# The chunk loop of an RWKV-7 recurrence, issued as eight pairs or as two groups of four

## The chip, the cores and the metric

The kernel runs on one NeuronCore of a Trainium2 chip. The metric is the device time of one execution in microseconds (us); lower is better. The engines that matter here are TensorE (PE, with its weight loads as PEld), VectorE (DVE), ScalarE (ACT), GpSimd (POOL) and the SyncE queue (SP), which issues the DMA transfers.

## The reference, cut to what matters

The model is a trunk of two layers on a sequence of 1024 positions with 1024 channels. Layer 0 mixes tokens with a chunked gMLP, layer 1 with RWKV-7 time mixing; each is followed by cross-attention into a memory and by a SwiGLU feed-forward block. The change touches only the recurrence of layer 1, for 16 heads of width 64:

```
def step(S, inp):                       # S: one 64 x 64 state for each head
    r_t, w_t, k_t, v_t, a_t, b_t = inp
    sa = einsum('bhij,bhj->bhi', S, a_t)
    S = S * w_t + sa (x) b_t + v_t (x) k_t
    return S, einsum('bhij,bhj->bhi', S, r_t)
...
y = rwkv7_recurrence(r, decay, k, v, -kk, kk * a)
y = group_norm(y) * ln_g + ln_b + sum(r * k * r_k) * v
out = (y * g) @ w_o
```

All inputs and outputs are 32-bit floats.

## The kernel before

The recurrence is computed in chunks of 64 positions. The 1024 positions are four *batches* of 256, so a batch has four chunks. Two heads share the 128 partitions and are called a *pair*, written `p`; there are eight pairs. Two pairs share their tiles and are called a *double*, written `pi`; there are four doubles. For each batch `b` there are five pieces of work, each written as a Python generator that yields between steps:

- **Preparation** (`rwkv_prep`, one call for each double): five loads from a scratch in DRAM, a scan of the decay (L1265), two exponentials (L1268, L1269), scaled operands `AR` and `BK` (L1277 to L1281, the last on POOL), a column of sums (L1288), 16 matmuls of the two operands (L1300) whose results are masked by DVE (L1303), eight transposes (L1307), the diagonal blocks stored to DRAM for the solve (L1313, L1314), a load of `v` (L1318) and 32 matmuls (L1324). Its products are four tiles `AR`, `GR`, `BT`, `UV` of the pool `A`.
- **Substitution** (`rwkv_solve`, one call for all eight pairs): a triangular inverse by forward substitution, 31 steps. Each step has one or two DVE operations (L1348), one DVE addition (L1345) and one POOL product (L1352) that need each other in turn. It begins with a load of the blocks that the preparation of all four doubles stored (L1336) and ends with stores to DRAM (L1357, L1360). Its tiles `invA` and `invZ` have one buffer each and are shared with the merge.
- **Merge** (`rwkv_merge`): loads the inverse back and joins its blocks by 32x32 matmuls (L1386, L1395) into the two tiles `Z`.
- **Chunk loop** (`rwkv_chunks`): 32 *units*, four chunks for each of eight pairs. A unit is: matmul of the state (L1422), DVE addition (L1423), matmul with `Z`, ACT copy (L1429), matmuls for the output and the new state (all recorded at L1409), ACT copy of the output (L1438) and ACT scaling of the state (L1441). The next chunk of the same pair needs the scaled state. Each unit holds one of the four PSUM banks of the pool `ck`, from its first matmul to its last copy.
- **Norm** (`rwkv_post`, one call for each double): mean, variance, scaling, transposes (L1496, L1503), gate, and a store of `z`.

The order in which the pieces are emitted is, for b = 1, 2: chunk loop of batch b-1; substitution of batch b; preparation of batch b+1 with the norm of batch b-1 ticking beside it; merge of batch b. For b = 3: chunk loop of batch 2, substitution of batch 3, then the output projection `W_o` begins; between its two column passes for the first half of the sequence come the merge of batch 3 and the chunk loop of batch 3.

The emitted order is not the order on the engines. The program is built with a planner (`schedule_with_timeline_sim=True`) that places every instruction into its engine's stream; an instruction emitted earlier has the higher priority, but one that the planner takes to be ready may be placed ahead of it. What stands in an engine's stream then runs in that order.

`stagger(gens, lag)` advances several generators in turn, the i-th from step `i * lag` on. `run` advances generators one after another and ticks the queued tasks (`later`) between steps; `drain` finishes the queued tasks.

Of the kernel before, what the change touches and what calls it, by code (L numbers as in the profile page):

```python
# [15 lines left out]
KD = D // P  # L16
# [5 lines left out]
class Trunk:  # L22
# [1375 lines left out]
            nc.scalar.copy(R['Z'][pi // 2][lo[pi], :, :, 32:64], pb[pi][lo[pi], :].rearrange('p (h c t) -> p h c t', h=2, c=8))  # L1398
            yield

    def rwkv_chunks(self, R, B, b, states):

        nc = self.nc
        heads = [slice(h * 64, h * 64 + 64) for h in range(2)]
        if b == 0:
            for p in range(KD):
                states[p] = R['st'].tile([P, P], F32, name='s', tag=f's{p}')
                nc.gpsimd.memset(states[p], 0.0)
        mm = lambda o, l, r: nc.tensor.matmul(o, lhsT=l, rhs=r, start=False, stop=True, skip_group_check=True)  # L1409

        def one(c4, p):
            pi, c = (p // 2, p % 2 * 4 + c4)
            T = B['T'][pi]
            AR, UV, BT, GR = (T['AR'], T['UV'], T['BT'], T['GR'])
            zr, to = (heads[pi % 2], heads[c % 2])
            bk = self.bank_ck()
            ar, u, sp = (bk[:, 0:128], bk[0:64, 128:256], bk[:, 256:384])
            s0 = states[p]
            last = b == 3 and c4 == 3
            rs = R['rs'][pi % 2][(p // 4 * 2 + p % 2) % 4]  # L1420
            uvc = UV[0:64, c].rearrange('i h v -> i (h v)')
            nc.tensor.matmul(ar, lhsT=AR[:, c, :, :], rhs=s0, start=True, stop=True)  # L1422
            nc.vector.tensor_add(rs[zr, :], ar[0:64, :], uvc)  # L1423
            if not last and False:
                nc.scalar.activation(s0, s0, AF.Copy, scale=T['D'][:, c:c + 1])
            yield
            for h, hs in enumerate(heads):
                mm(u[:, hs], R['Z'][pi // 2][:, h, c, :], rs[:, hs])
            nc.scalar.copy(uvc, u)  # L1429
            yield  # L1430
            if not last:
                mm(sp, self.ident, s0)
            for h, hs in enumerate(heads):
                mm(ar[64:128, hs], GR[:, h, c, :], UV[:, c, h, :])
            if not last:
                for h, hs in enumerate(heads[::-1]):
                    mm(sp[hs, hs], BT[:, c, hs], UV[:, c, hs.start // 64, :])
            e = lambda: nc.scalar.copy(AR[to, c - c % 2].rearrange('i a v -> i (a v)'), ar[64:128, :])  # L1438
            e()
            if not last:  # L1440
                nc.scalar.activation(s0, sp, AF.Copy, scale=T['D'][:, c:c + 1])  # L1441
            if not 1:
                e()
        order = sorted(((c4, p) for c4 in range(4) for p in range(KD)), key=lambda x: x[0] * 8 + x[1] + 1 * (x[1] // 2))
        if not 1:
            for c4, p in order:
                for _ in one(c4, p):
                    pass
                yield
            return  # L1450
        live = []
        for c4, p in order:
            live.insert(0, one(c4, p))
            live = [g for g in live if next(g, True) is None]
            yield
        while live:
            live = [g for g in live if next(g, True) is None]
            yield
# [50 lines left out]
    def rwkv(self, W, C, filler, mk_close):  # L1509
        nc = self.nc  # L1510
        B = [self.rwkv_batch() for _ in range(4)]
        R, states = ({}, {})
# [6 lines left out]
        def stagger(gens, lag):  # L1519

            gens = list(gens)
            done = [False] * len(gens)
            n = 0
            while not all(done):
                for i, g in enumerate(gens):
                    if n >= i * lag and (not done[i]):
                        try:
                            next(g)
                        except StopIteration:
                            done[i] = True  # L1530
                n += 1
                yield

        def prep(b):
            return stagger([self.rwkv_prep(R, B[b], pi, b, D_[0], C) for pi in range(4)], 7 if b else 6)

        def chunks(b):
            yield from self.rwkv_chunks(R, B[b], b, states)

        def post(b):  # L1540
            return stagger([self.rwkv_post(R, B[b], pi, b, D_[0], C) for pi in range(4)], 2 if b == 3 else 1)

        def run(*gens, rate=1):
            for g in gens:
                for _ in g:
                    self.tick(rate)

        def gated(half):

            xh, xl = self.chunks()  # L1550
            for k in range(KD):
                t = R['ld'].tile([P, 512], F32, name='zt', tag='ld')
                nc.sync.dma_start(t, D_[0]['z'][k, :, half * 512:half * 512 + 512])
                self.split(xh[k], xl[k], t)
            return (xh, xl)
        D_ = []

        def before_last():
            self.close_main()
            pools(left, 'left', ('inv', 1), ('D', 8))  # L1560
            self.rwkv_consts(left.enter_context(self.tc.tile_pool(name='rconst', bufs=1, reuse_waits='tile', side='left')), C)
            pools(left, 'left', ('ld', 7))
            pools(top, 'left', ('tt', 4))
            self.open_main(2, 3, 2)
            self.open_psum(4, 4)
            self.later(prep(0))
        d, gate_out = self.rwkv_project(W, C, filler, before_last, D_)
        self.drain()
        run(self.rwkv_solve(R, B[0]))
        p1 = prep(1)  # L1570
        self.later(p1)
        gate_out()
# [9 lines left out]
            nc.gpsimd.memset(z[96:128, :, :, 0:32], 0.0)  # L1582
        run(self.rwkv_merge(R, B[0]), p1)
        for b in range(1, 4):
            o = 3
            sv = self.rwkv_solve(R, B[b])
            if o in (0, 1):
                run(sv, chunks(b - 1))
            elif o in (2, 3):
                run(chunks(b - 1), sv)  # L1590
            else:
                self.later(sv)
                run(chunks(b - 1), rate=1)
                self.drain(0)
            self.later(post(b - 1), 1)
            if b == 3:
                break
            if o in (0, 2, 4):
                run(self.rwkv_merge(R, B[b]))
            run(prep(b + 1), rate=1)  # L1600
            if o in (1, 3, 5):
                run(self.rwkv_merge(R, B[b]))
            self.drain()
        top.close()
        self.open_main(2, 2, 1, 'left')
# [6 lines left out]
        x = gated(0)  # L1612

        def between():
            run(self.rwkv_merge(R, B[3]))
            self.drain()
            run(chunks(3))
            self.later(post(3), 1)
        first = self.out_half(x, 0, W['o'], close, 4, between)
        self.drain()  # L1620
        self.open_psum(8)
        x = gated(1)
# [82 lines left out]
```

## Time and profile before

| | us |
|---|---|
| median of three runs | 3295.14 (3293.02 to 3295.40) |
| the profiled execution, its own time | 3312.53 |
| span in its trace | 3310.8 |
| TensorE busy in the span | 3135.4 (95%) |
| VectorE busy | 2025.2 (61%) |
| ScalarE busy | 1490.8 (45%) |
| GpSimd busy | 1058.4 (32%) |

Mean granted TensorE clock over the span: 0.956 of full speed. The span runs from the first instruction to the last; the remaining 1.7 us of the execution's own time lie around it. Times inside the trace are counted from the span's start. The four chunk loops lie between 1884 and 2264 us. A busy TensorE is not a fast one: the column `PEclk` of the views tells which share of its full clock was granted, 1.00 for 2.4 GHz and 0.50 for 1.2 GHz.

### The profile page before, as it was taken

Reading aid. Unit: us, or ns where it says so; the run is one execution under the profiler, and the core shown is the slowest. Engines: PE = TensorE matmul, PEld = TensorE weight load, DVE = VectorE, ACT = ScalarE, POOL = GpSimd, SP = SyncE. Lnnn points to the kernel's source line nnn. Section 1 sums busy time; section 2 is a strip of 40 time slices with the busy share of each in tenths; the row PEclk is TensorE's granted clock in tenths of the full one; section 3 lists DMA queues with packets and bytes.
Section 4 is the critical chain, followed back from the end, with each engine's and each line's share of the span. In section 5 each row is a group of like instructions: output and inputs, shape, how many; then the busy total and the mean of one; then the engine's idle time right before and its main releaser. Section 6 shows DMA issues by size and latency. Waiting matters only on the chain. (4 is left out here: it accounts for less than half of the span.)

```text
span 3310.8 us, 44442 instructions
## 1 busy us (share of the span) xinstructions
PE 3135.4 (95%) x16570; PEld 2545.7 (77%) x16570; DVE 2025.2 (61%) x2876; ACT 1490.8 (45%) x2759; POOL 1058.4 (32%) x800
## 2 busy tenths in 40 slices
PE   8999999899999888999889899999999899999897
PEld 6888888778888666888667787887788688887676
DVE  5463545655444998755766567545545744445998
ACT  5443544533333433766743454445545533334332
POOL 0000011443334654311512244223011533334664
PEclk9999999999999999999999888779999999999998
DMA  5622544332222432744956644335554233323322
GB/s 186 204 77 70 197 147 141 114 96 83 77 77 85 144 102 77 238 136 131 301 173 169 169 121 100 105 92 176 178 163 150 65 96 86 86 77 120 103 96 96
DMA packets 448407, 421.97 MB, mean 127 GB/s; under 512 B 76672, under 2 KB 351264, under 8 KB 448192
## 3 DMA queue, kind: packets, MB, share of 16 engines
q1 hardware_dynamic: 441280, 393.96, 38.8%
q0 software_dynamic: 6912, 25.17, 2.4%
q8 instruction: 131, 2.15, 0.3%
q14 instruction: 84, 0.69, 0.1%
HBM read 314.13 MB, written 104.92 MB: 127 GB/s over the span
## 5 line engine op out<-in xcount | busy, mean ns | idle before, releaser
L438 PE MATMUL ps<-a,wh 128*128 128x512 f32 x2464 | 772.6, 399 | 6.1 <-DVE a L119 4.6
L119 DVE TENSOR_TENSOR wl<-wr,wh 128x1024 fp32r<-128x1024 f32 (+1 forms) x369 | 447.6, 1223 | 349.8 <-ACT wh L118 349.2
L438 PEld LDWEIGHTS ps<-a,wh 128*128 128x128 f32 x2464 | 465.6, 189 | 123.2 <-DVE a L119 7.0
L118 ACT CAST wh<-wr 128x1024 fp32r<-128x1024 f32 (+1 forms) x369 | 323.5, 889 | 522.4 <-PE ps L438 180.1
L438 PE MATMUL ps<-a,wl 128*128 128x512 f32 x1232 | 479.6, 397 | 0.0
L606 PE MATMUL ps<-wh,a 128*128 128x512 f32 x1136 | 380.3, 408 | 48.6 <-DVE a L615 32.6
L148 PE MATMUL ps<-a,wh 128*128 128x512 f32 (+1 forms) x848 | 330.3, 395 | 10.9 <-ACT a L118 5.9
L149 PE MATMUL ps<-a,wh 128*128 128x512 f32 (+1 forms) x848 | 325.7, 386 | 2.2 <-DVE a L119 2.2
L150 PE MATMUL ps<-a,wl 128*128 128x512 f32 (+1 forms) x848 | 325.4, 386 | 1.6 <-DVE wl L119 1.5
L148 PE MATMUL ps<-wh,a 128*128 128x512 f32 x800 | 313.9, 402 | 13.7 <-DVE a L1504 4.8
L149 PE MATMUL ps<-wl,a 128*128 128x512 f32 x800 | 318.5, 398 | 0.6 <-DVE wl L119 0.6
L150 PE MATMUL ps<-wh,a 128*128 128x512 f32 x800 | 316.7, 400 | 0.0
L606 PEld LDWEIGHTS ps<-wh,a 128*128 128x128 f32 x1136 | 218.9, 193 | 120.7 <-DVE a L615 32.5
L438 PEld LDWEIGHTS ps<-a,wl 128*128 128x128 f32 x1232 | 233.2, 189 | 57.6 <-DVE wl L119 0.8
L119 DVE TENSOR_TENSOR wl<-s,wh 128x512 fp32r<-128x512 f32 (+1 forms) x200 | 210.8, 1066 | 76.6 <-ACT wh L118 73.7
L118 ACT CAST wh<-s 128x512 fp32r<-128x512 f32 (+1 forms) x200 | 129.8, 662 | 251.0 <-PE ps L438 91.8
L606 PE MATMUL ps<-wl,a 128*128 128x512 f32 x568 | 228.8, 403 | 0.0
L208 POOL TENSOR_TENSOR sm<-sm,mhalf 128x4 f32<-128x4 f32 (+3 forms) x60 | 67.5, 1127 | 498.1 <-DVE sm L228 422.4
L119 DVE TENSOR_TENSOR a<-a 128x1024 fp32r<-128x1024 f32 (+1 forms) x134 | 208.1, 1567 | 24.3 <-ACT a L118 22.3
L615 DVE TENSOR_TENSOR a<-ps,a 128x512 f32<-128x512 f32 x304 | 194.8, 676 | 13.5 <-PE ps L606 13.4
L148 PEld LDWEIGHTS ps<-a,wh 128*128 128x128 f32 x848 | 163.3, 194 | 43.8 <-ACT a L118 6.8
L148 PEld LDWEIGHTS ps<-wh,a 128*128 128x128 f32 x800 | 151.9, 190 | 51.4 <-DVE a L1504 5.3
(273 smaller groups left out, 5631.7 us busy)
## 6 DMA issues: line engine op xcount, KB each, us to landing
wr<-in_ffn_w_in SPq DMA_DIRECT2D x90, 512.0 KB
scr<-t SPq DMA_DIRECT2D x136, 256.0 KB
scr<-t SPq DMA_DIRECT2D x60, 512.0 KB
a<-scr SPq DMA_DIRECT2D x108, 256.0 KB
wr<-in_rw_w_rkv SPq DMA_DIRECT2D x48, 512.0 KB
t<-scr SPq DMA_DIRECT2D x36, 512.0 KB
ld<-scr SPq DMA_DIRECT2D x72, 256.0 KB
wr<-in_xa_wkv SPq DMA_DIRECT2D x32, 512.0 KB
```

The source lines that it names most:

```text
L118: self.nc.scalar.copy(hi, src)
L119: (engine or self.nc.vector).tensor_sub(lo, src, hi)
L148: nc.tensor.matmul(out, lhsT=ah, rhs=bh, start=start, stop=False)
L149: nc.tensor.matmul(out, lhsT=ah, rhs=bl, start=False, stop=False)
L150: nc.tensor.matmul(out, lhsT=al, rhs=bh, start=False, stop=stop)
L208: self.nc.gpsimd.tensor_tensor(out=r, in0=v, in1=self.mhalf[:, 0:n], op=ALU.pow)
L438: self.nc.tensor.matmul(out, lhsT=a, rhs=b, start=start and k == 0 and (i == 0), stop=k == 3 and i == 2, skip_group_check=True)
L606: nc.tensor.matmul(ps, lhsT=a, rhs=b, start=start and k == 0 and (q == 0), stop=k == K - 1 and q == 2, skip_group_check=True)
L615: nc.vector.tensor_add(o, ps, o)
```

## The change

The chunk loop takes a group of four pairs (two doubles) and is called twice for each batch. The other work of the recurrence is emitted in turn with it, in halves of two doubles:

- With the first group of batch b-1, the preparation of doubles 2 and 3 of batch b (for b = 1 there is none, since batch 1 is already prepared).
- With the second group of batch b-1, the substitution of batch b, then side by side with it the norm of doubles 0 and 1 of batch b-1, followed by the preparation of doubles 0 and 1 of batch b+1.
- Then the norm of doubles 2 and 3 of batch b-1 is queued and the merge of batch b is emitted.
- For b = 3 whatever is left of substitution and norm when the second group ends is queued to run beside the output projection. Before the merge of batch 3 the queue is now drained first. The two groups of batch 3 are emitted in turn with each other.

No instruction's shape, engine or count changes.

```diff
+        pairs = range(4 * group, 4 * group + 4)
...
-        order = sorted(((c4, p) for c4 in range(4) for p in range(KD)), key=lambda x: x[0] * 8 + x[1] + 1 * (x[1] // 2))
+        order = [(c4, p) for c4 in range(4) for p in pairs]
...
+        def seq(*gens):
+            for g in gens:
+                yield from g
+        groups = [(0, 1), (2, 3)]
...
         for b in range(1, 4):
-            o = 3
             sv = self.rwkv_solve(R, B[b])
-                run(chunks(b - 1), sv)
-            self.later(post(b - 1), 1)
+            run(stagger([chunks(b - 1, 0), prep(b, groups[1]) if b > 1 else iter(())], 0))
+            ahead = prep(b + 1, groups[0]) if b < 3 else iter(())
+            rest = stagger([sv, seq(post(b - 1, groups[0]), ahead)], 0)
             if b == 3:
+                live = chunks(b - 1, 1)
+                for _ in live:
+                    next(rest, None)
+                self.later(rest)
+                self.later(post(b - 1, groups[1]), 1)
                 break
-            run(prep(b + 1), rate=1)
-                run(self.rwkv_merge(R, B[b]))
+            run(stagger([chunks(b - 1, 1), rest], 0))
+            self.later(post(b - 1, groups[1]), 1)
+            run(self.rwkv_merge(R, B[b]))
             self.drain()
...
         def between():
+            self.drain()
             run(self.rwkv_merge(R, B[3]))
-            self.drain()
-            run(chunks(3))
+            run(stagger([chunks(3, g) for g in range(2)], 0))
             self.later(post(3), 1)
```

## Rows read from the trace of the kernel before

**Rows 1.** Page, the span in 40 slices: TensorE busy tenths and granted clock tenths

```profile
PE   8999999899999888999889899999999899999897
...
PEclk9999999999999999999999888779999999999998
```

**Rows 2.** Busy time by stretch; after ACT and POOL: clock, DMA share, GB/s

```profile
core 0: us, PE busy (x) PEld busy (x) DVE busy (x) ACT busy (x) POOL busy (x), PEclk, DMA share, GB/s
1892.00:1942.00 50.00, 49.47 (x632) 41.12 (x629) 38.06 (x139) 32.44 (x108) 23.95 (x35) 1.00 0.30 79
1942.00:1966.00 24.00, 24.00 (x210) 20.78 (x211) 13.39 (x25) 9.63 (x19) 12.24 (x11) 0.51 0.40 114
1966.00:2002.00 36.00, 36.00 (x382) 32.05 (x381) 24.80 (x55) 16.68 (x43) 7.12 (x6) 1.00 0.62 167
2002.00:2038.00 36.00, 34.91 (x359) 27.86 (x358) 27.80 (x109) 21.31 (x71) 17.92 (x30) 1.00 0.18 51
2038.00:2075.00 37.00, 30.52 (x260) 25.31 (x258) 23.36 (x53) 13.28 (x31) 16.36 (x13) 0.50 0.62 148
...
2089.00:2120.00 31.00, 31.00 (x229) 27.17 (x228) 8.61 (x22) 6.56 (x13) 0.00 (x0) 0.50 0.44 122
2120.00:2165.00 45.00, 43.45 (x464) 35.37 (x465) 34.38 (x128) 29.32 (x96) 21.16 (x33) 1.00 0.27 78
2198.00:2232.00 34.00, 34.00 (x367) 28.93 (x364) 5.13 (x15) 11.89 (x35) 2.08 (x2) 0.51 0.18 55
1892.00:2120.00 228.00, 219.90 (x2236) 186.51 (x2233) 143.19 (x418) 104.82 (x291) 82.79 (x99) 0.80 0.43 115
```

**Rows 3.** Timeline of TensorE: start, us, engine, line, operation, tiles, count

```profile
1943.35 2.08 PE L1300 MATMUL ps<-ar,bk 64*128 64x128 f32 x8
2075.56 1.15 PE L1324 MATMUL ps<-uv,bk 128*64 128x64 f32 x16
2077.88 1.05 PE L1288 MATMUL ps<-sel,ld 128*128 128x2 f32 x8
2078.86 1.71 PE L1300 MATMUL ps<-ar,bk 64*128 64x128 f32 x16
2080.68 0.66 PE L1307 MATMUL ps<-ident,bk 128*128 128x128 f32 x4
2194.16 0.60 PE L1496 MATMUL ck<-ident,a 128*128 128x128 f32 x4
```

**Rows 4.** Timeline of VectorE: first substitution step of batch 1, while its chunk loop runs

```profile
1893.96 0.36 DVE L1348 SCALAR_TENSOR_TENSOR invZ<-invZ,invA 128x1 f32<-128x1 f32 x2 [4.39 <-DMA invA<-scr]
```

**Rows 5.** Busy time of L1422 alone by stretch (TensorE, weight loads, clock)

```profile
1900.00:1930.00 30.00, 9.56 (x42) 6.10 (x42) 1.00 0.15 41
...
1966.00:2002.00 36.00, 3.29 (x18) 2.35 (x17) 1.00 0.62 167
```

**Rows 6.** Groups of VectorE by line, 1890 to 2120 us: two substitutions

```profile
L1348 DVE SCALAR_TENSOR_TENSOR invZ<-invZ,invA 128x1 f32<-128x1 f32 (+30 forms) x122 | 32.9, 301 | 6.3 <-DMA invA<-scr 5.7
L1345 DVE TENSOR_TENSOR invZ<-invZ,invP 128x29 f32<-128x29 f32 (+14 forms) x58 | 19.5, 336 | 0.3 <-POOL invP L1352 0.2
L1423 DVE TENSOR_TENSOR rs<-ck,uv 64x128 f32<-64x128 f32 x60 | 16.7, 281 | 17.6 <-PE ck L1422 16.9
```

**Rows 7.** Timeline of VectorE: substitution of batch 2, steps 1, 26 and 31

```profile
2007.14 0.42 DVE L1348 SCALAR_TENSOR_TENSOR invZ<-invZ,invA 128x1 f32<-128x1 f32 x2 [1.34 <-DMA invA<-scr]
...
2032.14 0.36 DVE L1348 SCALAR_TENSOR_TENSOR invZ<-invZ,invA 128x26 f32<-128x26 f32 x1
...
2045.29 0.27 DVE L1348 SCALAR_TENSOR_TENSOR invZ<-invZ,invA 128x31 f32<-128x31 f32 x1
```

**Rows 8.** Timeline of TensorE: waits around the end of that substitution

```profile
2037.77 0.59 PE L1409 MATMUL ck<-rs,z 128*64 128x64 f32 x4 [0.92 <-DVE rs L1423]
...
2056.58 1.08 PE L1386 MATMUL ck<-x 32*32 32x32 f32 x58 [5.85 <-DMA x<-scr]
```

**Rows 9.** Timeline of TensorE: merges of batches 1 and 3

```profile
1937.26 1.54 PE L1386 MATMUL ck<-x 32*32 32x32 f32 x46
...
2196.38 2.04 PE L1386 MATMUL ck<-x 32*32 32x32 f32 x62 [1.18 <-ACT a L1500]
```

**Rows 10.** Timeline of the SP queue: loads that begin the substitutions of batches 2 and 3

```profile
2003.67 0.34 SPq L1336 DMA_DIRECT2D invA<-scr  x1
...
2117.26 0.34 SPq L1336 DMA_DIRECT2D invA<-scr  x1
```

More of the change, by code (lines that the diff above doesn't have):

```diff
@@ L1399, in rwkv_merge, with rwkv_chunks @@
             yield
-    def rwkv_chunks(self, R, B, b, states):
+    def rwkv_chunks(self, R, B, b, states, group):
         nc = self.nc
         heads = [slice(h * 64, h * 64 + 64) for h in range(2)]
+        pairs = range(4 * group, 4 * group + 4)
         if b == 0:
-            for p in range(KD):
+            for p in pairs:
                 states[p] = R['st'].tile([P, P], F32, name='s', tag=f's{p}')
@@ L1443, in one @@
                 e()
-        order = sorted(((c4, p) for c4 in range(4) for p in range(KD)), key=lambda x: x[0] * 8 + x[1] + 1 * (x[1] // 2))
[L1445 to L1450, printed above, removed]
+        order = [(c4, p) for c4 in range(4) for p in pairs]
         live = []
@@ L1532, in stagger, with prep, chunks, post @@
                 yield
[L1534 to L1541, printed above, removed]
+        def prep(b, pis=range(4)):
+            return stagger([self.rwkv_prep(R, B[b], pi, b, D_[0], C) for pi in pis], 7 if b else 6)
+        def chunks(b, group):
+            return self.rwkv_chunks(R, B[b], b, states, group)
+        def post(b, pis=range(4)):
+            return stagger([self.rwkv_post(R, B[b], pi, b, D_[0], C) for pi in pis], 2 if b == 3 else 1)
+        def seq(*gens):
+            for g in gens:
+                yield from g
+        groups = [(0, 1), (2, 3)]
         def run(*gens, rate=1):
@@ L1584, in rwkv @@
         for b in range(1, 4):
-            o = 3
             sv = self.rwkv_solve(R, B[b])
-            if o in (0, 1):
-                run(sv, chunks(b - 1))
-            elif o in (2, 3):
-                run(chunks(b - 1), sv)
[L1591 to L1594, printed above, removed]
-            self.later(post(b - 1), 1)
-            if b == 3:
-                break
-            if o in (0, 2, 4):
-                run(self.rwkv_merge(R, B[b]))
-            run(prep(b + 1), rate=1)
-            if o in (1, 3, 5):
-                run(self.rwkv_merge(R, B[b]))
+            run(stagger([chunks(b - 1, 0), prep(b, groups[1]) if b > 1 else iter(())], 0))
+            ahead = prep(b + 1, groups[0]) if b < 3 else iter(())
+            rest = stagger([sv, seq(post(b - 1, groups[0]), ahead)], 0)
+            if b == 3:
+                live = chunks(b - 1, 1)
[3 more added lines that the diff above has]
+                self.later(post(b - 1, groups[1]), 1)
+                break
+            run(stagger([chunks(b - 1, 1), rest], 0))
+            self.later(post(b - 1, groups[1]), 1)
+            run(self.rwkv_merge(R, B[b]))
             self.drain()
```

## Prediction

> **What bounds the kernel now.** I read the page's 40 slices first [rows 1]: TensorE is busy throughout, and the one place where its granted clock sags is slices 24 to 28, the recurrence. The change touches only that place, so I cut it into stretches by the clock [rows 2]. The reader is to see three things there. TensorE is busy nearly always: 219.9 of the 228 us from 1892 to 2120. Its clock is at one of two levels, 1.00 or 0.50, for long stretches: half clock for 24 us from 1942, 37 us from 2038, 31 us from 2089 and 34 us from 2198. And VectorE is far from full over the whole, 143.2 of 228 us, but unevenly loaded: 27.8 of 36 us where a substitution runs beside the chunk loop, 8.6 of 31 us where only preparation is left.
>
> So the stage is bound by TensorE's instruction stream, and what it loses is mainly clock. That half clock really costs is seen in the timeline [rows 3]: eight records of the preparation's matmuls take 2.08 us at half clock, and sixteen take 1.71 us at full clock. A stretch of L us that is busy at half clock therefore gives back about L/2 if it runs at full clock.
>
> What stands before the falls? Before 1942 and before 2198 come the 32x32 matmuls of a merge [rows 9], the latter after an idle 1.18 us. Before 2038 TensorE waits 0.92 us for VectorE [rows 8]. The fall at 2089 comes as the merge thins out into bare preparation. What holds full clock: chunk units alone (2002 to 2038, 2120 to 2165) and chunk units mixed with preparation (1966 to 2002, where TensorE is never idle) [rows 2]. Chunk units alone don't bring the clock back quickly, though: the loop of batch 3 runs at half clock from the merge to 2232.
>
> One more view limits what a new order of emission can do. The first substitution step of batch 1 runs at 1893.96 [rows 4], although it is emitted after the whole chunk loop of batch 0, which ends some 45 us later. The planner already moves ready work into idle engines. Emission sets priorities, and buffers and data do the rest.
>
> **The change part by part.** No instruction is added or removed; only places change, so every term below is a difference in waiting or in clock. First the sizes of the pieces on TensorE at full clock. In 30 us of pure chunk loop there are 42 records of L1422, two for a unit [rows 5]: 21 units, 1.43 us each; a group's 16 units take 22.9 us, a batch's 45.7. Preparation of one double is 32 records of L1300 (2 x 1.71), 8 of L1307 (2 x 0.66), 32 of L1324 (2 x 1.15) and L1288 (1.05) [rows 3]: 8.1 us. Norm of one double is 0.60 for L1496 and as much for L1503 [rows 3]: 1.2 us.
>
> *Eight pairs to groups of four.* The next chunk of a pair now comes four units later instead of eight. I cost this at nothing: only four `ck` banks exist, and a unit's bank comes free with the scaling of the state that the next chunk waits for. The distance of four is already there. If the cover were gone, the loss would show as idle TensorE before L1422. In the mixed stretch, where units come at 9 in 36 us [rows 5], there was none.
>
> *Preparation of doubles 2 and 3 beside the first group.* 22.9 + 16.2 = 39.1 us on TensorE, all of it mixed work of the kind that held full clock from 1966 to 2002. This removes the stretch where preparation runs bare, 2089 to 2120: 31 us busy at half clock, worth **15.5 us**. From below: nothing, if the clock falls in the mix as well. From above: 15.5 us, since the work itself stays. I take 15.5, because its nearest row is the mixed stretch at 1.00.
>
> *The load that starts a substitution* (L1336) needs the preparation of all four doubles. It was issued at 2003.67 and 2117.26, right where preparation ended [rows 10]. Batch 2's came 66 us after its preceding merge began at 1937.26 [rows 9]. Afterwards it can come some 8 us of merge plus 39 us later, so no later than now. Behind it on SP stand loads for the norm and for the next preparation; I cost these at 0 to 3 us, hidden behind 22.9 us of the second group's units.
>
> *Substitution of batch 2 beside the second group, with norm and preparation.* Here VectorE gets crowded. Two substitutions took 32.9 + 19.5 us [rows 6], so 26.2 each; 16 chunk additions of 0.281 take 4.5. From the 143.2 us of VectorE in 1892 to 2120 [rows 2] I take off the three lines of rows 6 (69.1): 74.1 us for eight preparations and eight norms, 9.3 for one of each, 18.5 for two. Sum 49.2 us, against 22.9 + 16.2 + 2.4 = 41.5 us on TensorE. The price is thus between 0 (other TensorE work, norm and preparation of the other doubles, fills in) and 7.7 us. I take 0 for the likeliest, since the planner did lift such work before [rows 4], and keep 7.7 for the rival. Batch 1's substitution is ready from the start and lies beside the first group too; batch 3's has no preparation beside it and `W_o` behind it. Both at nothing.
>
> The Trainium skill ("TensorE: Matmul & The Clock Gate", section "Architectural detail") says that VectorE and ScalarE take their instructions strictly in order, while TensorE can only pull weight loads ahead. By that rule a substitution step waits behind every norm or preparation operation that stands before it, and the sum would be that of the VectorE rival below. This trace agrees at one spot, the 2.6 us steps described there.
>
> *Merges and the loop of batch 3.* Three merges remain, alone or with norm beside them, so the falls at 1942 and 2198 and the stretches behind them (24 and 34 us) stay. The stretch from 2038 (37 us) also holds a merge, its norms and preparation; the wait of 5.85 us for the merge's load [rows 8] stays as well. I change none of these. Draining before merge 3 moves a few norm operations ahead of the merge's loads, beside the projection's matmuls: nothing.
>
> **Sum and cross-check.** -15.5 us. Independently, TensorE's work for one period from merge to merge is 8 for the merge (62 records of its 128 matmuls, two records each, take 2.04 us [rows 9]) + 45.7 + 32.4 + 4.8 = 91 us. The period before was 2056.58 - 1937.26 = 119 us [rows 8, 9]. With one half-clock stretch behind the merge (12 to 18 us) and 6 us of waiting, the new one is 109 to 115 us. The first of the two periods thus gains 4 to 10 us and the second about as much, 8 to 20 together; 15.5 lies inside.
>
> The profiled execution took 3312.5 us, 17.4 more than the median of the runs, 3295.1. A difference carries over: 3295.1 - 15.5 = 3279.6, so I predict 3280. A measurement of this kernel tells about 0.2% (6.6 us) from no change.
>
> **Rivals.**
> *More of the half clock goes.* If mixed work also brings the clock back sooner, the stretches from 1942 and 2038 shrink as well. All of both would be 24/2 + 30.5/2 + 6.5 idle = 33.8 us more: 3246. For it: 1966 to 2002. Against it: both falls follow merges or waits that stay. Half of it is 3263; I put this case at 3246 to 3270.
>
> *Nothing comes of it.* TensorE has the same records to run, was idle 8 us of 228, and the planner reorders anyway. The bare preparation could drop out and a new half-clock stretch of about 30 us appear, behind a merge or between the two halves. Then 3295. For it: recovery took 24 to 37 us every time [rows 2], whatever ran.
>
> *VectorE's stream takes over (slower).* Place: the second group of batch 2, lines L1348 and L1345. From step 1 to 26 the substitution of batch 2 took 25.0 us, 1.0 us a step; then norm and preparation entered VectorE's stream, and the next five steps took 13.2 us, 2.6 each [rows 7]. There TensorE waited 0.92 us for L1423 [rows 8], and the clock fell. The change puts such a mix beside all 31 steps. Price: 7.7 us of VectorE excess and one more half-clock stretch like that from 2038, 37/2 = 18.5, less the 15.5 gained: +10.7, so 3306. It decides from where a step takes over 41.5/31 = 1.34 us on average. Against it: from 1966 to 2002 VectorE was busy 24.8 of 36 us with preparation and unit additions, and TensorE was never idle [rows 2].
>
> **Chances and range.** The likeliest, 0.42: 3280, own range 3272 to 3288. More clock: 0.15, around 3258. Nothing: 0.18, 3289 to 3301. VectorE: 0.25, around 3306, up to 3314 if batch 3's merge waits as well. Faster by over 0.2% is the first two, 0.57; same 0.18; slower 0.25. The range 3254 to 3310 leaves out the better half of the second case and the tail of the last.
>
> **What would show it.** Right: no stretch of bare preparation, and clock 1.00 wherever chunk units and preparation alternate; three half-clock stretches of 24 to 37 us, each behind a merge; substitution of batch 2 at under 1.34 us a step; merge to merge 109 to 115 us. Wrong on the slow side: TensorE waits for L1423 in the second group, steps near 2 us, half clock in the mixed stretches. Wrong on the fast side: clock back within some 10 us of a merge. A difference after 2264 us, where nothing is changed, would be a cause I left out.

## Result and profile after

| | changed kernel, first timing | changed kernel, second timing (e16) | profiled execution of the first |
|---|---|---|---|
| time, us | 3318.27 median (8 runs) | 3308.33 median (12 runs) | 3317.83, span 3316.1 |
| kernel before beside it, us | 3295.27 | 3298.87 | 3312.53, span 3310.8 |
| ratio | 1.0065 [1.0041, 1.0090] | 1.0032 [1.0011, 1.0054] | |

The change makes the kernel slower, by 0.3 to 0.6%: 10 to 21 us where 15.5 us of gain were forecast. The profiled execution of before was itself 17 us above its median, so the spans of the two traces differ by 5.3 us only, and a difference between two traces is no measure of the change. Of the 5.3 us, 4.2 lie in the recurrence: from the first load L1336 to the start of the last unit's copy it took 2263.5 - 1795.3 = 468.2 us before and 2269.6 - 1797.2 = 472.4 us after. Behind it nothing changed (1047.3 and 1046.5 us).

The line numbers of the changed kernel: state matmul L1423 (was L1422), its addition L1424, chain matmuls L1410, a unit's copy L1439, the norm's GpSimd scaling L1484, its transposes L1491 and L1498. Preparation, substitution and merge keep theirs.

The page's slices, as in [rows 1]:

```profile
PE   8999999899999888999889999899999899999897
...
PEclk9999999999999999999999798779999999999999
```

The stretches of the recurrence cut by the granted clock, columns as in [rows 2]:

```profile
1892.00:1962.00 70.00, 67.34 (x780) 56.56 (x781) 55.27 (x175) 39.61 (x122) 29.36 (x40) 0.99 0.45 114
1962.00:1975.00 13.00, 12.30 (x211) 11.58 (x201) 4.98 (x10) 8.04 (x15) 10.64 (x10) 0.50 0.31 80
1975.00:1999.00 24.00, 24.00 (x235) 20.24 (x235) 10.44 (x26) 11.40 (x35) 2.15 (x2) 0.99 0.43 126
1999.00:2020.00 21.00, 21.00 (x117) 16.84 (x118) 6.65 (x16) 5.71 (x17) 0.19 (x1) 0.51 0.24 64
2020.00:2071.00 51.00, 47.80 (x496) 40.16 (x496) 43.99 (x134) 28.24 (x82) 29.38 (x34) 1.00 0.42 115
2071.00:2105.00 34.00, 22.34 (x341) 20.93 (x342) 18.38 (x52) 9.77 (x18) 12.29 (x16) 0.50 0.54 127
```

The reader is to see that the forecast stretch of bare preparation (2089 to 2120 in [rows 2]) is gone, and the 24 us behind the merge of batch 1 are down to 13. Two other stretches are to be explained: 21 us at half clock from 1999, in the very mix of chunk units and preparation that was to hold full clock, and 34 us from 2071, in which TensorE is idle for a third of the time; it answers to the 37 us from 2038 in [rows 2].

Between these two traces the clock gives back what was forecast: up to 2105 us TensorE is busy at half clock for 12.3 + 21.0 + 22.3 = 55.6 us, against 24.0 + 30.5 + 31.0 = 85.5 us up to 2120 in [rows 2], though before's trace is one with a low clock. What grew is TensorE's idle time. Over the whole recurrence, in before, the changed kernel and the changed kernel's second trace (e16), columns as above:

```profile
1795.30:2263.80 468.50, 444.83 (x4360) 373.28 (x4359) 274.67 (x788) 218.06 (x589) 160.22 (x210) 0.84 0.42 116
```

```profile
1797.20:2269.90 472.70, 438.25 (x4360) 366.38 (x4359) 276.38 (x787) 219.56 (x588) 158.03 (x209) 0.85 0.41 115
```

```profile
1790.40:2253.30 462.90, 429.27 (x4360) 359.47 (x4359) 278.04 (x787) 220.00 (x588) 157.86 (x209) 0.87 0.43 117
```

TensorE is idle for 23.7, 34.5 and 33.6 us of these spans. The largest single wait lies where the 34 us begin, in this stretch of TensorE's timeline, which answers to [rows 8] (start, us, what it waited for):

```profile
2067.57 1.03 PE L1324 MATMUL ps<-uv,bk 128*64 128x64 f32 x14 [0.22 <-DVE bk L1303]
2078.92 1.11 PE L1491 MATMUL ps<-ident,a 128*128 128x128 f32 x4 [10.32 <-POOL a L1484]
...
2095.22 1.93 PE L1386 MATMUL ck<-x 32*32 32x32 f32 x128 [2.98 <-DMA x<-scr]
```

TensorE stands 10.32 us behind a transpose of the norm, whose operand GpSimd scales late. GpSimd's own timeline shows why it is late:

```profile
2069.01 1.15 POOL L1474 TENSOR_TENSOR a<-a,bo 128x512 f32<-128x512 f32 x1
2072.37 1.24 POOL L1352 TENSOR_TENSOR invP<-invZ,invA 128x161 f32<-128x161 f32 x1 [2.20 <-DVE invZ L1348]
2073.71 1.64 POOL L208 TENSOR_TENSOR sm<-sm,mhalf 128x8 f32<-128x8 f32 x1
2075.31 0.89 POOL L1352 TENSOR_TENSOR invP<-invZ,invA 128x144 f32<-128x144 f32 x2
2076.16 1.70 POOL L208 TENSOR_TENSOR sm<-sm,mhalf 128x8 f32<-128x8 f32 x1
2077.83 1.04 POOL L1484 TENSOR_TENSOR a<-a,sm 128x512 f32<-128x512 f32 x1
```

Between the norm's operations stand products of the substitution (L1352), and these wait for VectorE. Norm and substitution take turns in the streams of VectorE and GpSimd. The substitution itself now takes from 2023.65 to 2084.62, 61 us for 31 steps, where it took 38 us in [rows 7]:

```profile
2023.65 0.34 DVE L1348 SCALAR_TENSOR_TENSOR invZ<-invZ,invA 128x1 f32<-128x1 f32 x2
...
2084.62 0.27 DVE L1348 SCALAR_TENSOR_TENSOR invZ<-invZ,invA 128x31 f32<-128x31 f32 x1
```

Its load and that of batch 3, which answer to [rows 10], came 12.7 and 6.1 us later than before:

```profile
2016.34 0.34 SPq L1336 DMA_DIRECT2D invA<-scr  x1
...
2123.41 0.34 SPq L1336 DMA_DIRECT2D invA<-scr  x1
```

The Trainium skill ("TensorE: Matmul & The Clock Gate", section "Architectural detail") says that VectorE takes its instructions strictly in order and that TensorE can only pull weight loads ahead. This trace agrees: for 10.32 us TensorE did nothing of what stood behind L1491, although the operand of the matmuls L1288 there had been written by 2064.5:

```profile
2063.60 0.87 DVE L1285 SCALAR_TENSOR_TENSOR ld<-ld,pcol,lx 128x256 f32<-128x256 f32 x2
```

```profile
2082.39 1.71 PE L1288 MATMUL ps<-sel,ld 128*128 128x2 f32 x8
```

### The profile page after: what moved, and what is told of

Same layout as the page of the kernel before. It is cut to its first block, busy times and chain, and to the rows that moved or that the text cites. A ratio compares the mean times of both kernels' runs of the same rounds, so it can differ in the third digit from the quotient of the medians.

```text
span 3316.1 us, 44443 instructions
## 1 busy us (share of the span) xinstructions
PE 3130.7 (94%) x16570; PEld 2538.7 (77%) x16570; DVE 2024.3 (61%) x2876; ACT 1492.5 (45%) x2759; POOL 1053.7 (32%) x800
## 3 DMA queue, kind: packets, MB, share of 16 engines
q1 hardware_dynamic: 441280, 393.96, 38.7%
## 5 line engine op out<-in xcount | busy, mean ns | idle before, releaser
L606 PEld LDWEIGHTS ps<-wh,a 128*128 128x128 f32 x1136 | 218.1, 192 | 119.0 <-DVE a L615 36.4
L438 PEld LDWEIGHTS ps<-a,wl 128*128 128x128 f32 x1232 | 233.2, 189 | 57.6 <-DVE wl L119 0.9
L119 DVE TENSOR_TENSOR wl<-s,wh 128x512 fp32r<-128x512 f32 (+1 forms) x200 | 219.0, 1107 | 76.1 <-ACT wh L118 73.4
L119 DVE TENSOR_TENSOR a<-a 128x1024 fp32r<-128x1024 f32 (+1 forms) x134 | 193.8, 1461 | 26.3 <-ACT a L118 22.6
L150 PEld LDWEIGHTS ps<-a,wl 128*128 128x128 f32 x848 | 163.5, 193 | 36.3 <-DVE wl L119 2.9
```

The source lines that it names most:

```text
L119: (engine or self.nc.vector).tensor_sub(lo, src, hi)
L150: nc.tensor.matmul(out, lhsT=al, rhs=bh, start=False, stop=stop)
L438: self.nc.tensor.matmul(out, lhsT=a, rhs=b, start=start and k == 0 and (i == 0), stop=k == 3 and i == 2, skip_group_check=True)
L606: nc.tensor.matmul(ps, lhsT=a, rhs=b, start=start and k == 0 and (q == 0), stop=k == K - 1 and q == 2, skip_group_check=True)
```

## Experiments

All ratios are to the kernel before, timed on the same chip beside it, with a 95% interval. Where two experiments are set against each other, the difference of the means of their runs stands with twice its standard error. The diffs are cut to the lines that matter. In e1, e9, e11 and e12 the merge of batch 3 also comes ahead of the drain again, as before; in the others it stays behind it.

**First question: does the mix beside the substitution cost the time?** That was theory S. Its rival G: the groups of four do.

**e1**, groups alone; the order of emission is that of before, the two groups run one after the other.

```diff
-            run(stagger([chunks(b - 1, 0), prep(b, groups[1]) if b > 1 else iter(())], 0))
...
+            run(chunks(b - 1, 0)); run(chunks(b - 1, 1)); run(sv)
+            self.later(post(b - 1), 1)
+            run(prep(b + 1), rate=1)
+            run(self.rwkv_merge(R, B[b]))
```

> Only the grouping: the chunk loop of a batch runs as two groups of four pairs one after the other, and everything else is emitted in the order of the kernel before. Theory S (the norm and preparation beside the substitution of batch 2 slow it and hold up TensorE): the grouping is innocent, 1.000 of the kernel before (0.998 to 1.002), substitution of batch 2 at about 1 us a step. Rival G (the shorter distance between two chunks of a pair starves TensorE): 1.004 to 1.008, with TensorE idle before the state's matmul in the pure chunk stretches.

Measured 3308.79, ratio 1.0039 [1.0010, 1.0068]. Grouping alone costs. In its trace the first substitution is longer. VectorE's groups during it (1894 to 1931 us):

```profile
L1424 DVE TENSOR_TENSOR rs<-ck,uv 64x128 f32<-64x128 f32 x24 | 6.6, 280 | 2.8 <-PE ck L1423 2.5
L1473 DVE TENSOR_TENSOR a<-ar,sm 128x512 f32<-128x512 f32 x2 | 1.4, 684 | 0.0
L1469 DVE TENSOR_REDUCE sm<-ar 128x8 f32<-128x512 f32 x2 | 1.3, 670 | 0.0
...
L1482 DVE TENSOR_REDUCE sm<-ps 128x8 f32<-128x512 f32 x1 | 0.7, 683 | 0.0
L1279 DVE TENSOR_TENSOR ar<-lx,tt 128x512 f32<-128x512 f32 x1 | 0.7, 673 | 0.0
```

In the same view of before, VectorE runs nothing but the substitution and L1423 until the substitution ends. With groups, doubles 0 and 1 are done halfway through the loop, their norm is ready, and the planner lifts it and part of a preparation into the substitution: that takes 37.1 us instead of 28.7 (first step to last). The starving that rival G expected is small: in the recurrence TensorE waits 2.4 us ahead of the state's matmul, against 0.9 before. That the longer substitution is what costs isn't shown: the traces of e1 and of before took 3313.91 and 3312.53 us, so they don't hold the loss.

**e2, e3, e4**, changed kernel with the two additions beside the substitution taken out, one or both, and emitted behind it: e2 leaves the substitution alone with the second group, e3 keeps only the norm there, e4 only the preparation.

```diff
-            rest = stagger([sv, seq(post(b - 1, groups[0]), ahead)], 0)
+            rest = sv                                       # e2
+            rest = stagger([sv, post(b - 1, groups[0])], 0) # e3
+            rest = stagger([sv, ahead], 0)                  # e4
```

> The changed kernel, but beside the second group stands the substitution alone; norm and the preparation of doubles 0 and 1 of the next batch are emitted behind it, as in the kernel before. The preparation of doubles 2 and 3 stays beside the first group. Theory S: the loss goes, 0.994 to 1.001 of the kernel before, substitution of batch 2 back to 33 to 40 us, no idle of several us on TensorE before the norm's transposes. Rival G: it stays at 1.004 to 1.008. Rival C (the loss is only a matter of where half-clock stretches fall): anything from 0.995 to 1.008, with the time following the mean clock and not the length of the substitution.

> The changed kernel, but only the norm of doubles 0 and 1 stands beside the substitution; the preparation of doubles 0 and 1 of the next batch comes behind it. If the norm is what hurts (its scaling runs on GpSimd between the substitution's products, and TensorE's transposes wait for it): 1.004 to 1.007. If the preparation is what hurts (it fills VectorE): 0.996 to 1.001. Substitution of batch 2: about 45 us in either case, against 33 to 38 in the kernel before and 65 in the changed one.

> The changed kernel, but only the preparation of doubles 0 and 1 of the next batch stands beside the substitution; all norms of the batch are queued behind it. If the preparation is what hurts: 1.004 to 1.008, substitution of batch 2 at 50 us or more. If the norm is: 0.996 to 1.001, and TensorE has no 10 us of idle before the norm's transposes while the substitution runs.

Measured 1.0119 [1.0086, 1.0151], 1.0125 [1.0096, 1.0154] and 1.0021 [0.9995, 1.0048]. e2 and e3 lie outside every range that was expected. Theory S falls as the whole account: with less beside the substitution the kernel gets slower, and preparation beside it is worth 28.5 ± 9.6 us (e2 to e4, mean of the runs). What S says of the steps isn't refuted by this: preparation that leaves the substitution must run elsewhere, and the load of the second substitution comes late there (first legs in the table below). e2 and e3 are alike: in e2 too, the planner lifts the norm into the second substitution.

**e7**, the changed kernel with the norm's two GpSimd products on VectorE.

```diff
-        E = lambda n: nc.gpsimd if n in (('vt', 'yr', 'zg', 'sub') if last else ('vt', 'yr')) else nc.vector
+        E = lambda n: nc.gpsimd if n in (('vt', 'yr', 'zg', 'sub') if last else ()) else nc.vector
```

> The changed kernel, but the two products of the norm that ran on GpSimd (the gates vt and the scaling yr of batches 0 to 2) run on VectorE. If the wait of 10.3 us in which TensorE stands behind L1491 for GpSimd's L1484 is GpSimd's own queue (products of the substitution and the power of the norm ahead of it), it goes, and the kernel takes 3306 to 3312 us (ratio 1.003 to 1.005). If VectorE's stream beside the substitution is the limit, the two products lengthen it and the wait stays or grows: 3318 us or more (1.0065 to 1.009).

Measured 1.0099 [1.0083, 1.0116]. The wait doesn't go; TensorE's waits from 1880 to 2275 (total, times, longest) name VectorE in GpSimd's place:

```profile
PE ps L1491 <- DVE a L1484: 7.6, 2, 6.6
PE ck L1491 <- DVE sm L202: 6.0, 1, 6.0
```

So the wait isn't GpSimd's own queue alone: with the scaling on VectorE, TensorE waits there for VectorE.

**Second question: where should the second half of the preparation stand?** Theory C (not the rival C in e2's expectation): what costs is that doubles 2 and 3 are prepared in turn with the first group, called the cut below. The units that run meanwhile delay the load of the next substitution and are then missing as TensorE's work beside it.

**e6, e8, e9** have the preparation of doubles 0 and 1 beside the substitution and the norms behind, like e4. e6 runs the loop over eight pairs (its halves are the first and last 16 units), e8 keeps the groups but prepares doubles 2 and 3 ahead of the merge, e9 does both.

```diff
-            run(stagger([chunks(b - 1, 0), prep(b, groups[1]) if b > 1 else iter(())], 0))
+            run(chunks(b - 1, 0))                    # e8; e9: the first 16 units of eight pairs
...
             self.later(post(b - 1), 1)
+            run(prep(b + 1, groups[1]), rate=1)      # e8, e9
             run(self.rwkv_merge(R, B[b]))
```

> As e4 (preparation of the next doubles 0 and 1 beside the second half, of doubles 2 and 3 beside the first half, all norms behind; e4 took 1.0021), but the chunk loop runs over all eight pairs in the order of before, and its halves are the first and the last 16 units. If grouping by four costs what it cost alone (e1: 1.0039, or 6 us at an equal clock), this run stands 0.2 to 0.4% below e4: 0.998 to 1.000, about 3289 to 3296 us. If grouping costs only where the loop runs with nothing else to fill TensorE, it stands at e4's 1.001 to 1.003.

> As e4, but the preparation of doubles 2 and 3 of the next batch isn't left for the following first group: it runs behind the second group, ahead of the merge, as before, so that the next substitution can be loaded ahead of the next chunk loop. If leaving the second half of the preparation to the next loop is what delays the substitutions (e2 and e3 stand at 1.012), this run stands below e4 at 0.995 to 0.999, 3280 to 3292 us, and substitution of batch 3 starts at about 2117 us as before instead of e4's 2129. If the delay costs nothing and the loss is grouping, the bare preparation comes back with its half clock and it takes 3298 to 3308 us (1.001 to 1.004).

> Before with one thing moved: the preparation of the next doubles 0 and 1 is emitted in turn with the substitution and the last 16 units of the loop over eight pairs; doubles 2 and 3, the norms and the merge stay behind it as before. If preparation beside the substitution is worth what e4 gained on e2 (1.0%), and grouping and the cut are the costs, this is the best order: 0.993 to 0.998, 3273 to 3289 us. If preparation in the mix only moves the half clock elsewhere, it takes what before takes: 0.999 to 1.001, 3292 to 3299 us.

Measured 1.0022 [1.0003, 1.0041], 0.9998 [0.9976, 1.0020] and 0.9960 [0.9944, 0.9976]. e9 beats both kernels by more than its interval. Between e8 and e9 lie 12.5 ± 6.2 us, the price of grouping once more (and of the drain's place, for which e12 shows no price); between e4 and e6, on two chips, it doesn't show. Between e6 and e9 lie 19.4 ± 6.5 us: the place of the second half.

**e10, e13** test theory C from two sides. e10 is the changed kernel, norm and preparation beside the substitution as they were, with doubles 2 and 3 ahead of the merge as in e8. e13 is e6, where doubles 2 and 3 stay behind the merge but are emitted ahead of the loop and not in turn with it.

```diff
-            run(stagger([half, prep(b, groups[1]) if b > 1 else iter(())], 0))
+            run(prep(b, groups[1]) if b > 1 else iter(()))   # e13
+            run(next(live) for _ in range(16))
```

> The changed kernel, but the preparation of doubles 2 and 3 of the next batch runs behind the second group and ahead of the merge, not beside the following first group; norm and preparation of doubles 0 and 1 stay beside the substitution. With e8 (no norm there) it gives the price of the norm without the cut, with the changed kernel the price of the cut. If the two prices add (norm 0.44% from the changed kernel and e4, e8 at 0.9998): 1.003 to 1.005, 3304 to 3311 us. If the norm costs by itself and the cut nothing: 1.0055 to 1.0075. If the norm costs only together with the cut: 0.999 to 1.001.

> e6 (loop over eight pairs, the preparation of doubles 2 and 3 left for the next loop), but that preparation is emitted ahead of the first half of the loop instead of in turn with it. If what costs in the cut is that the load of the next substitution (L1336) waits for a preparation spread over the first half, it comes some 20 us sooner here and the kernel takes 0.996 to 0.999, 3281 to 3291 us. If the preparation behind a merge costs because it then runs alone at half clock, it takes 1.002 to 1.005, 3301 to 3311 us.

Measured 0.9985 [0.9966, 1.0004] and 0.9960 [0.9942, 0.9977]. Both agree with C in the time. In e13 the load came 10 us sooner behind the merge than in e6, not 20. The norm beside the substitution costs nothing in e10, against the price that I had taken from e4; the expectation that prices add was wrong.

**e11**, e9 with three doubles beside the substitution and one behind.

```diff
-        groups = [(0, 1), (2, 3)]
+        groups = [(0, 1, 2), (3,)]
```

> e9 with three doubles of the next preparation beside the second half of the loop over eight pairs and one behind it. If each double moved into the mix saves bare preparation at half clock (e9: two doubles, 0.4%), three save 0.5 to 0.7%: 0.993 to 0.995, 3271 to 3278 us. If VectorE's stream is the limit, as in the changed kernel, the third double lengthens the substitution's steps and it takes 0.997 to 1.002, 3284 to 3301 us.

Measured 1.0184 [1.0156, 1.0212], far outside both expectations. The load of batch 2 and, further on, TensorE's wait ahead of merge 3:

```profile
2052.98 0.34 SPq L1336 DMA_DIRECT2D invA<-scr  x1
```

```profile
2251.11 2.05 PE L1386 MATMUL ck<-x 32*32 32x32 f32 x128 [22.07 <-DMA x<-scr]
```

All 32 units of the loop have run when this load comes, so nothing of the loop is left beside the substitution. That is theory C at its extreme: in the second leg (load to merge 2, 58.0 us) TensorE is idle for 19.6 us. Why the last double was prepared so late (from 2030 us, among the norms) wasn't tested.

**e12**, the changed kernel with the end as before: substitution of batch 3 behind the second group, all norms of batch 2 behind it, merge 3 ahead of the drain.

```diff
             if b == 3:
-                live = chunks(b - 1, 1)
-                for _ in live:
-                    next(rest, None)
-                self.later(rest)
-                self.later(post(b - 1, groups[1]), 1)
+                run(chunks(b - 1, 1), sv)
+                self.later(post(b - 1), 1)
                 break
```

> The changed kernel, but what comes behind the last preparation is as before: substitution of batch 3 emitted behind the second group, all norms of batch 2 behind it, merge 3 ahead of the drain, and the last loop's groups one after the other. Batches 1 and 2 are as in the changed kernel. If the loss sits in batch 2's second group (the 10.3 us for which TensorE stood behind L1491), this changes little: 1.005 to 1.007, 3310 to 3318 us. If a good part sits in batch 3 (merge 3 came some 8 us later than before, with norm beside the third substitution), 1.002 to 1.004, 3301 to 3308 us.

Measured 1.0056 [1.0033, 1.0079]: as the first expectation had it, and within the changed kernel's own two intervals. No loss at the end shows, to within some 7 us either way.

**e14, e15, e16**: one line of the changed kernel moved, each way, and the changed kernel again.

```diff
-            run(stagger([chunks(b - 1, 0), prep(b, groups[1]) if b > 1 else iter(())], 0))
+            run(prep(b, groups[1]) if b > 1 else iter(()))   # e14; e15 has these two the other way round
+            run(chunks(b - 1, 0))
```

> The changed kernel with one line moved: the preparation of doubles 2 and 3 is emitted ahead of the first group, not in turn with it; both stay behind the merge, and everything else is as in the changed kernel. If the loss comes from the units that TensorE runs ahead of the load of the next substitution (11 in the changed kernel's batch 2, 3 in e10's), the load of batch 2 comes at about 2000 us instead of 2016 and the kernel takes 0.996 to 1.001, 3282 to 3299 us. If the loss is in the norm and the preparation beside the substitution, which are unchanged, it stays at 1.005 to 1.008, 3311 to 3322 us.

> The same line moved the other way: the whole first group is emitted ahead of the preparation of doubles 2 and 3. By the theory of the units ahead of the load, all 16 units of the group run ahead of it, it comes at 2020 to 2030 us, and the kernel is slower than the changed one: 1.010 to 1.017, 3327 to 3350 us. By the theory of the crowded substitution nothing changes: 1.005 to 1.008.

> The changed kernel once more, on the same chip as the two runs beside it: 1.004 to 1.009 by its own earlier interval. Its second trace tells whether the late load (2016 us), the long second substitution (61 us) and TensorE's wait behind L1491 return. By the theory of the units ahead of the load all three do; if the wait behind L1491 was a chance of one execution, it is under 3 us here.

Measured 1.0004 [0.9982, 1.0026], 1.0029 [1.0006, 1.0052] and 1.0032 [1.0011, 1.0054]. Moving the line forward gives back 13.8 ± 5.2 us (e16 to e14). Moving it back changes nothing, against the expectation of theory C. The traces tell why: e15 has 11 units between the merge and the load like the changed kernel, nearly the same substitution (60.5 us) and 9.93 us behind L1491. The planner had made nearly the same order of both. In e16 the late load and the long substitution (60.7 us) return, and so does the wait:

```profile
2063.22 1.11 PE L1491 MATMUL ps<-ident,a 128*128 128x128 f32 x4 [9.53 <-POOL a L1484]
```

How e14's trace differs, by stretches from merge to load to merge to load to merge (merge 1, load 2, merge 2, load 3, merge 3, by their batch); first the changed kernel, then e14:

```profile
1955.80:2016.30 60.50, 58.14 (x643) 49.40 (x642) 27.73 (x64) 25.89 (x65) 13.15 (x12) 0.75 0.40 107
2016.30:2095.20 78.90, 64.81 (x587) 55.39 (x587) 62.65 (x186) 34.58 (x95) 40.20 (x47) 0.82 0.42 111
2095.20:2123.40 28.20, 27.43 (x435) 23.53 (x436) 5.20 (x16) 11.63 (x29) 2.06 (x3) 0.82 0.57 151
2123.40:2200.10 76.70, 70.40 (x574) 56.51 (x574) 57.21 (x156) 44.28 (x120) 33.80 (x42) 0.98 0.36 101
```

```profile
1957.00:2000.30 43.30, 39.68 (x559) 35.36 (x559) 24.86 (x57) 20.59 (x45) 13.05 (x12) 0.88 0.60 152
2000.30:2066.80 66.50, 57.63 (x611) 48.43 (x610) 55.81 (x175) 35.81 (x109) 35.56 (x45) 0.96 0.43 115
2066.80:2098.80 32.00, 31.98 (x454) 29.16 (x455) 12.28 (x30) 11.24 (x25) 4.13 (x5) 0.71 0.60 169
2098.80:2182.80 84.00, 74.97 (x622) 59.95 (x620) 59.49 (x162) 47.51 (x132) 35.09 (x41) 0.97 0.35 100
```

Load 2 comes 17 us sooner after the merge, the way from it to merge 2 is 12 us shorter and the clock in it is 0.96 instead of 0.82. Idle time of TensorE over the four stretches is nearly the same (23.5 and 21.5 us), since e14 waits 8.1 us for the load of merge 2 where the changed kernel waits behind L1491; in these two traces the gain is mostly clock. They don't measure the 13.8 us, though: e14's execution (3300.65 us) took as long as the one traced in e16 (3301.26), against whose legs the two are 11 and 10 us shorter and the last, to merge 3, 7 us longer. The units that run ahead of that substitution's load and beside it, by the copies L1439 (one a unit, the bracketed number), in the changed kernel and in e14:

```profile
1955.80:2016.30 60.50, 2.88 (x11) 0.75 0.40 107
```

```profile
2016.30:2085.30 69.00, 5.50 (x21) 0.87 0.36 101
```

```profile
1957.00:2000.30 43.30, 1.06 (x4) 0.88 0.60 152
```

```profile
2000.30:2056.20 55.90, 7.31 (x28) 1.00 0.35 100
```

All kernels together, from their traces, in us. The first leg runs from merge 1 to the load of substitution 2, the second from there to merge 2; VectorE is its busy time in the second leg. The steps are those of substitution 2, and the units are batch 1's ahead of its load and beside it. Each trace is one execution, up to 23 us from its kernel's median (e4).

| kernel | ratio | first leg | second leg | VectorE | sum | steps | units |
|---|---|---|---|---|---|---|---|
| before | 1 | 66.4 | 52.9 | 41.7 | 119 | 38.1 | 7, 24 |
| changed | 1.0065 | 60.5 | 78.9 | 62.7 | 139 | 61.0 | 11, 21 |
| e16, changed again | 1.0032 | 54.6 | 76.2 | 63.3 | 131 | 60.7 | 12, 20 |
| e15 | 1.0029 | 60.4 | 78.3 | 62.0 | 139 | 60.5 | 11, 21 |
| e14 | 1.0004 | 43.3 | 66.5 | 55.8 | 110 | 52.1 | 4, 28 |
| e10 | 0.9985 | 44.8 | 67.9 | 57.3 | 113 | 51.5 | 3, 27 |
| e8 | 0.9998 | 49.6 | 60.8 | 49.3 | 110 | 43.6 | 6, 22 |
| e9 | 0.9960 | 64.2 | 52.4 | 44.6 | 117 | 39.1 | 6, 24 |
| e13 | 0.9960 | 60.4 | 50.2 | 41.9 | 111 | 38.7 | 8, 24 |
| e6 | 1.0022 | 70.5 | 57.6 | 48.0 | 128 | 43.0 | 11, 21 |
| e12 | 1.0056 | 60.9 | 77.4 | 63.2 | 138 | 60.5 | 11, 21 |
| e7 | 1.0099 | 54.0 | 75.9 | 64.9 | 130 | 60.3 | 12, 20 |
| e1 | 1.0039 | 67.7 | 51.8 | 41.2 | 119 | 38.3 | 4, 25 |
| e4 | 1.0021 | 56.5 | 52.3 | 45.7 | 109 | 39.1 | 15, 17 |
| e2 | 1.0119 | 79.5 | 62.8 | 51.2 | 142 | 48.7 | 9, 23 |
| e3 | 1.0125 | 75.4 | 70.4 | 58.0 | 146 | 53.4 | 8, 24 |
| e11 | 1.0184 | 110.5 | 58.0 | 40.0 | 168 | 41.4 | 32, 0 |

But for e1, every kernel whose interval lies above 1 has a long leg: the first (70 us and more) where the load comes late, the second (75 us and more) where the substitution takes 60 us. The kernels with a sum of 109 to 117 are all within 0.21% of before or faster.

The count of units doesn't order the kernels. e3 and e13 have the same 8 and 24, and they are 1.65% apart; e6 has the changed kernel's 11 and 21 with a substitution of 43.0 us; e4 has only 17 beside the substitution and the shortest sum. What the second leg does follow, in all kernels but e11, is VectorE's busy time in it: the leg takes 1.14 to 1.27 times as long. A longer leg has room for more of VectorE's work too, so this doesn't tell which comes first. The second leg of e13:

```profile
2002.84:2053.04 50.20, 47.85 (x535) 40.70 (x534) 41.91 (x147) 28.38 (x88) 20.35 (x33) 1.00 0.34 98
```

So the two comparisons that move the cut alone (e16 to e14, e6 to e13) show its price, but not that missing units are how it acts: in both, VectorE's work in the second leg falls too (63.3 to 55.8 and 48.0 to 41.9 us). No run changes one of the two alone.

## Why the prediction was wrong

**The step that failed** is the preparation of doubles 2 and 3 beside the first group. I priced it by the clock alone, at -15.5 us, and what it does to the substitution behind it at nothing. By e14 this one line costs 13.8 ± 5.2 us. I checked that its load would come "no later than now", and counted from its merge that held: 60.5 us against 66.4. I had both sides of the account of the second group, 49.2 us of VectorE against 41.5 us of TensorE, and took the price as 0, on the reason that the planner fills in. It did fill in, but with more work for VectorE, from doubles 2 and 3 and the next batch: VectorE was busy for 62.7 us from the load to merge 2. The lines L1482 (one a norm) and L1277 (one a preparation) count it, here during the second substitution of the changed kernel and then of e14:

```profile
L1277 DVE SCALAR_TENSOR_TENSOR ar<-ld,tt 128x504 f32<-128x504 f32 x3 | 2.9, 954 | 0.0
...
L1482 DVE TENSOR_REDUCE sm<-ps 128x8 f32<-128x512 f32 x4 | 2.7, 680 | 0.0
```

```profile
L1482 DVE TENSOR_REDUCE sm<-ps 128x8 f32<-128x512 f32 x2 | 1.4, 676 | 0.0
...
L1277 DVE SCALAR_TENSOR_TENSOR ar<-ld,tt 128x504 f32<-128x504 f32 x2 | 1.3, 670 | 0.0
```

By these lines four norms and three preparations went into the one, two of each into the other, and the substitution came to 61 and 52.1 us. 21 units lie beside the one, 28 beside the other. For eight pairs e6 and e13 show the price of the line again, 20.9 ± 6.6 us (on two chips; 22.9 when each is taken against the kernel before beside it).

**Grouping costed at nothing** was wrong too. By e1 it costs 0.39% [0.10, 0.68], by e8 and e9 12.5 ± 6.2 us. I looked for it in TensorE's idle time ahead of L1422, where little of it is. With groups the first substitution takes longer, 37.1 us in e1 and 43.2 in e8 against 28.7 before and 28.3 in e9, as other work goes between its steps: mostly norm in e1, mostly preparation in e8. That this is the price isn't shown.

**The gain from bare preparation** came, but by another move: e9 puts doubles 0 and 1 beside the substitution and gains 0.40% [0.24, 0.56], 13 us. The 15.5 us were forecast for doubles 2 and 3 beside the first group, so that the sizes are close is in part luck. From merge 2 to load 3 e9's clock is 0.78, against 0.61 before. Grouping (+13), the line of e14 (+14) and this gain (-13) come to about +14 us, within the measured 10 to 21; the step that is left out, from e8 to e14, is -1 us.

**Mixed work holds full clock** was wrong as a rule: 1999 to 2020 in the changed kernel is such a mix with TensorE never idle, at 0.51. In e16 the first leg holds 0.91. What decides it stays open.

**The VectorE rival** named the place, the second group of batch 2, and the signs: steps near 2 us (61/31 = 1.97), TensorE waiting, half clock behind it. Its time, 3306, was 2 to 12 us short, and near in part by luck: it adds a half-clock stretch, while in the trace half clock fell and idle time grew. It also looked for the wait at L1423, and it was at the norm's transpose. Its threshold of 1.34 us a step doesn't hold: e10 and e14 take 1.66 and 1.68 and lose nothing against before, with 27 and 28 units beside them. The runs neither show the crowding as the cause by itself nor exclude it.

**What held:** merge to merge in 109 to 115 us is what e10, e13 and e14 show (113, 111, 110), not the changed kernel (139 and 131). The end of the loop and the drain show no cost in e12. After 2264 us nothing changed.

**Still open:** why e4 and e6 show no price of grouping, and how much of the changed kernel's 10 to 21 us is which, and whether the cut acts by missing units or by VectorE's work; the two timings of the same kernel differ as much as their intervals allow.

## What to carry to other kernels

When a load waits for the last piece of a preparation and starts a long chain on another engine, try that piece undiluted ahead of the work that is to cover the chain: here that was worth 14 us with groups and 21 with eight pairs. Before moving work into a chain's cover, set the chain's own engine time against what is left beside it, and let a surplus count as a price, not as something that the planner fills. Count then, in a trace, what the planner really put between the chain's steps: an order that makes some work ready sooner can crowd the chain, though no emission puts it there, and two orders of emission can come out nearly the same (e15, e16).

## What the runs showed of the hardware

Time follows the mean granted clock from run to run of one and the same kernel: before took 3276.40 us at 0.968 and 3310.24 at 0.955 among the 23 runs beside e1 to e4. This spread of 1% with no change in the code is larger than most effects here; with twelve runs a side the difference of two kernels still had an interval of 5 to 6 us each way. In the changed kernel the stretch at half clock from 1999, with TensorE busy throughout (21.0 of 21.0 us), is of this kind: the same code held 0.91 from merge 1 to load 2 in e16, against 0.75.

During a wait of 10 us TensorE's clock fell to half and stayed there for 34 us (2071 to 2105), in which it was busy for 22.3 us. An estimate from these figures: at full clock that work would have taken half, so the clock cost about 11 us beside the 10 us of idle time. Not all of it is the wait's, since before the merge of batch 2 ran at half clock too ([rows 2], 2038 to 2075).
